# Two transformer blocks in split float32: which engine computes the weights' low parts, and how the account that orders the program treats VectorE and GpSimd

## The chip, the cores and the metric

One NeuronCore of a Trainium2 chip runs the whole program in one launch. The metric is the device time of one execution in microseconds (us), as the median of several runs. TensorE (PE) multiplies matrices, VectorE (DVE), ScalarE (ACT) and GpSimd (POOL) work elementwise, SyncE (SP) issues the transfers. Each engine takes its own instructions in the order in which the program lists them and waits on semaphores where it needs another's result. The program is unrolled: the order is fixed when the kernel is built.

## The reference

The input is 256 tokens of width 1024, float32. Two blocks of two layers follow each other; each layer is a SwiGLU feed-forward part (FFN, inner width 2816), a mixer, and a second FFN, each with an RMS norm ahead and a residual sum behind.

```python
for l in range(DEPTH):
    x = x + 0.5 * swiglu(rmsnorm(x, ffn1_norm[l]), ffn1_w_in[l], ffn1_w_out[l])
    x = x + hybrid_mixer(rmsnorm(x, mix_norm[l]), w_in[l], ...)
    x = x + 0.5 * swiglu(rmsnorm(x, ffn2_norm[l]), ffn2_w_in[l], ffn2_w_out[l])
```

The mixer of block 1 has two branches of 8 heads of 128: a gated delta rule in chunks of 64 tokens (a triangular system per chunk, then a state carried from chunk to chunk) and stick-breaking attention; each is multiplied by a branch matrix and gated, and their sum goes through `w_out`. The mixer of block 2 has three attention branches (latent, block-sparse, dilated). Every weight is used once, on all 256 tokens.

## The kernel before

**Split matmuls.** A float32 product is made of three one-pass matmuls: each operand is split into a high part `hi`, its rounding to TensorE's one-pass type, and a low part `lo = x - hi`; `mm3` issues hi·hi, hi·lo and lo·hi. So every weight that comes in (`raw`, by SP's transfers, four buffers) needs two elementwise instructions for each piece of 128x512 (some are narrower): the rounding `hi<-raw`, on ScalarE or VectorE, and the subtraction `lo<-raw,hi`. `Stream.split` (line 336) does it seven pieces ahead of their use (`PIECE_AHEAD`), into nine buffers. There are 1752 pieces. In `Net.split` (line 529) a table of costs decides the engines: the subtraction goes to GpSimd where that is reckoned to end earlier than on VectorE, or before TensorE's own time plus a slack: 7 us in the block-1 mixers (`POOL_SLACK`, line 21, set at lines 636 and 1491), 5 us at the end of an FFN (`EDGE_SLACK`, lines 22 and 679), 0 elsewhere. Data in PSUM (tiles `dn`, `acc`) never go to GpSimd.

**Dense and background work.** `dense` and `dense_tok` (one chunk of 256 weight columns, eight steps of 6 matmuls, 48 in all, into `dn` banks) are the program's thread. The mixers' chains, `delta` and `stick` in block 1, `soft2` and `soft3` in block 2, are generators that yield between steps; a step is some TensorE work into an `acc` bank and what the other engines do with it. After each eighth of a chunk `between` calls `tick` (line 492):

```python
if q and max(self.due.get(id(q), 0.0), self.nc.bank_free("acc", 4)) <= self.nc.free["tensor"]:
    self.step(q)
```

`due` is the time at which the chain's last step ends by the account in `Clock` (lines 233 to 289). The account keeps a time for each engine; it books each instruction behind its engine's last one, its inputs and its buffer, at the price of `cost`. So the account decides after how many dense matmuls a chain's next step stands in TensorE's queue. Where the program needs a chain's result, `need` and `drain` (lines 498 and 503) emit what is left of it at once, with no dense matmul between.

**A mixer of block 1** is 48 chunks: the columns for four pairs of heads (`dq`, `dk`, `dv`, `z`, `sq`, `sk`, `sv`, with the gates `ga` between), `gb`, then the branch matrices `yb` (four chunks, whose input `ob` needs all of `stick`: line 848) and `ya` (four chunks, input `oa`, all of `delta`: line 856), then `wo`. There are four `delta` chains in two lanes and four `stick` chains in one. By its dense matmuls the first mixer falls into four stages: pairs 0 and 1 (14 chunks), pairs 2 and 3 with the gates before them (16), the last gate, `z`, `gb` and `yb` (10), `ya` and `wo` (8).

Of the kernel before, what the change touches and what calls it, by code (L numbers as in the profile page):

```python
# [8 lines left out]
F = mybir.dt.float32  # L9
# [11 lines left out]
POOL_SLACK = 7.0  # L21
EDGE_SLACK = 5.0
# [210 lines left out]
class Clock:  # L233
    def __init__(self, nc):
        self.nc = nc
        self.free = {"tensor": 0.0, "vector": 0.0, "scalar": 0.0, "gpsimd": 0.0}
        self.ready = {}
        self.used = {}
        self.avail = {}
        self.slots = {}  # L240
        self.last = 0.0
        for n in self.free:
            setattr(self, n, Engine(self, n, getattr(nc, n)))
        self.sync = nc.sync
# [28 lines left out]

    def ends(self, eng, op, out, ins):

        at = max([self.free[eng], self.avail.get(out.tensor.name, 0.0)] + [self.ready.get(a.tensor.name, 0.0) for a in ins])
        return at + self.cost(eng, op, out, ins)

    def account(self, eng, op, aps, kw):
        out, ins = aps[0], aps[1:]  # L280
        cost = self.cost(eng, op, out, ins)
        at = max([self.free[eng], self.avail.get(out.tensor.name, 0.0)] + [self.ready.get(a.tensor.name, 0.0) for a in ins])
        end = at + cost
        self.free[eng] = end
        for a in aps:
            self.used[a.tensor.name] = end + 0.1
        self.ready[out.tensor.name] = end + (0.07 if eng == "tensor" else 0.13)
        if eng != "tensor":
            self.last = max(self.last, end + 0.13)
# [95 lines left out]
class Net:  # L385
    def __init__(self, ctx, tc, x, wsrc, small, out, parts):
# [16 lines left out]
        self.pool_slack = 0.0  # L403
# [125 lines left out]
    def split(self, hi, lo, x, gain=None):  # L529

        nc = self.nc
        if gain is None:
# [4 lines left out]
            psum = x.tensor.name.startswith(("dn_", "acc"))  # L537
            eng = "vector"
            if not psum and nc.ends("gpsimd", "tensor_sub", lo, [x, hi]) < max(
                    nc.ends("vector", "tensor_sub", lo, [x, hi]), nc.free["tensor"] + self.pool_slack):  # L540
                eng = "gpsimd"
            getattr(nc, eng).tensor_sub(lo, x, hi.bitcast(F))
# [82 lines left out]
    def dense(self, key, xs, mid=None):  # L625
# [10 lines left out]
        self.pool_slack = self.slack  # L636
# [35 lines left out]
    def ffn(self, part, nxt):  # L672
        nc = self.nc
# [3 lines left out]
        def out(c):  # L677
            if c == 10:
                self.pool_slack = EDGE_SLACK
# [804 lines left out]
    def run(self):  # L1484
        parts = self.parts
        for i, p in enumerate(parts):
# [4 lines left out]
            self.slack = POOL_SLACK if p[:2] == (1, "mix") else 0.0  # L1491
# [101 lines left out]
```

## Time and profile before

| | us |
|---|---|
| median of 3 runs (lowest, highest) | 2856.28 (2854.34, 2857.47) |
| the profiled execution, its own time | 2855.17 |
| its span, first to last instruction | 2853.4 |
| one mixer of block 1 (two of them) | 412.7 and 412.6 |
| one mixer of block 2 (two of them) | 262 |
| one FFN (eight of them) | 184 |

Times in the trace are counted from the span's start. A row's busy time is that in which an engine worked on an instruction; an engine whose instruction waits for a semaphore is idle, one whose instruction has begun is busy, whether it makes headway or not. All elementwise instructions pass through one helper and bear its line, 228, so they are told apart by their tiles. The granted clock is TensorE's, as a share of 2.4 GHz.

### The profile page before, as it was taken

Reading aid. Unit: us, or ns where it says so; the run is one execution under the profiler, and the core shown is the slowest. Engines: PE = TensorE matmul, PEld = TensorE weight load, DVE = VectorE, ACT = ScalarE, POOL = GpSimd, SP = SyncE. Lnnn points to the kernel's source line nnn. Section 1 sums busy time; section 2 is a strip of 40 time slices with the busy share of each in tenths; the row PEclk is TensorE's granted clock in tenths of the full one; section 3 lists DMA queues with packets and bytes.
Section 4 is the critical chain, followed back from the end, with each engine's and each line's share of the span. In section 5 each row is a group of like instructions: output and inputs, shape, how many; then the busy total and the mean of one; then the engine's idle time right before and its main releaser. Section 6 shows DMA issues by size and latency. Waiting matters only on the chain.

```text
span 2853.4 us, 57792 instructions
## 1 busy us (share of the span) xinstructions
PE 2701.7 (95%) x22692; PEld 2654.9 (93%) x22692; DVE 2067.7 (72%) x3749; ACT 1389.5 (49%) x2761; POOL 751.2 (26%) x625
## 2 busy tenths in 40 slices
PE   8997888999999978889999999899999999899998
PEld 8997887999999978889999999889999999889998
DVE  6678889476676688894766767766766767767766
ACT  5444454544454444545444544455544544545543
POOL 0016555770010265557600101322000002321000
PEclk9998999999999989999999999999999999999999
DMA  6553233345555532233455555434555554435553
GB/s 222 185 170 133 101 107 118 132 171 200 191 189 187 171 125 104 104 119 134 170 205 188 202 190 176 153 127 156 192 187 196 185 187 164 139 129 178 192 192 126
DMA packets 128146, 463.48 MB, mean 162 GB/s; under 512 B 14336, under 2 KB 14592, under 8 KB 127744
## 3 DMA queue, kind: packets, MB, share of 16 engines
q1 hardware_dynamic: 127872, 459.78, 47.5%
q8 instruction: 178, 2.92, 0.4%
q14 instruction: 96, 0.79, 0.1%
HBM read 458.67 MB, written 1.05 MB: 161 GB/s over the span
## 4 chain that ended last, share of the span: by engine, by line
PE 74%; DVE 20%; ACT 3%; issue 2%; DMA 1%; POOL 0%; DVEq 0%; SPq 0%; ACTq 0%; POOLq 0%
PE dn L228 53%; PE acc L228 21%; DVE ssum L228 2%; DVE lo L228 1%; DVE xl L228 1%; DVE d_N L228 1%; DVE hi L228 1%; DVE dq L228 1%; DVE dv L228 1%; DVE dk L228 1%; DVE d_prod L228 1%; DVE d_dec L228 1%; DVE d_Ub L228 1%; DVE d_P L228 1%; DMA raw<-in_w_dram 1%
## 5 line engine op out<-in xcount | busy, mean ns | idle before, releaser
L228 POOL TENSOR_TENSOR lo<-raw,hi 128x512 fp32r<-128x512 f32 (+2 forms) x502 | 665.2, 1345 | 1791.4 <-DVE lo L228 843.5
L228 ACT ACTIVATE hi<-raw 128x512 fp32r<-128x512 f32 (+2 forms) x1562 | 895.6, 617 | 333.3 <-PE dn L228 205.0
L228 DVE TENSOR_TENSOR lo<-raw,hi 128x512 fp32r<-128x512 f32 x1250 | 841.2, 710 | 166.9 <-ACT hi L228 155.9
L228 PE MATMUL dn<-xh,hi 128*128 128x256 f32 x4208 | 852.6, 284 | 6.0 <-DVE hi L228 6.0
L228 PE MATMUL dn<-xl,hi 128*128 128x256 f32 x4208 | 834.0, 280 | 4.1 <-DVE xl L228 4.1
L228 PE MATMUL dn<-xh,lo 128*128 128x256 f32 x4208 | 832.0, 279 | 4.7 <-DVE lo L228 4.7
L228 PEld LDWEIGHTS dn<-xh,hi 128*128 128x128 f32 x4208 | 647.3, 191 | 16.5 <-issue 9.1
L228 PEld LDWEIGHTS dn<-xl,hi 128*128 128x128 f32 x4208 | 646.7, 191 | 5.9 <-DVE xl L228 5.9
L228 PEld LDWEIGHTS dn<-xh,lo 128*128 128x128 f32 x4208 | 645.0, 191 | 5.5 <-DVE lo L228 5.5
L228 PE MATMUL acc<-al,hi 128*128 128x256 f32 x1408 | 204.3, 282 | 0.0
L228 PE MATMUL acc<-ah,hi 128*128 128x256 f32 x1408 | 202.8, 281 | 0.0
L228 PE MATMUL acc<-ah,lo 128*128 128x256 f32 x1408 | 202.8, 281 | 0.0
L228 ACT ACTIVATE ah<-us 128x512 fp32r<-128x512 f32 x88 | 55.7, 632 | 283.4 <-DVE us L228 283.4
L228 PEld LDWEIGHTS acc<-ah,lo 128*128 128x128 f32 x1408 | 183.0, 189 | 0.0
L228 PEld LDWEIGHTS acc<-al,hi 128*128 128x128 f32 x1408 | 183.0, 189 | 0.0
L228 PEld LDWEIGHTS acc<-ah,hi 128*128 128x128 f32 x1408 | 181.5, 188 | 0.0
L228 ACT ACTIVATE gs<-gs 128x512 f32<-128x512 f32 x88 | 55.9, 635 | 227.3 <-DVE gs L228 227.3
L228 PE MATMUL dn<-hi,xh 128*128 128x256 f32 (+2 forms) x640 | 139.7, 300 | 2.5 <-DVE k L228 2.5
L228 DVE TENSOR_TENSOR gs<-dn,nr 128x512 f32<-128x512 f32 x88 | 60.8, 691 | 103.1 <-PE dn L228 102.9
L228 DVE TENSOR_TENSOR us<-dn,nr 128x512 f32<-128x512 f32 x88 | 60.7, 690 | 102.7 <-PE dn L228 102.7
L228 PE MATMUL dn<-lo,xh 128*128 128x256 f32 (+2 forms) x640 | 130.8, 286 | 2.9 <-DVE lo L228 2.9
L228 PE MATMUL dn<-hi,xl 128*128 128x256 f32 (+2 forms) x640 | 130.9, 286 | 0.0
(319 smaller groups left out, 3234.2 us busy)
## 6 DMA issues: line engine op xcount, KB each, us to landing
raw<-in_w_dram SPq DMA_DIRECT2D x853, 512.0 KB, 4.3
raw<-in_w_dram SPq DMA_DIRECT2D x14, 384.0 KB, 3.2
raw<-in_w_dram SPq DMA_DIRECT2D x4, 408.0 KB, 4.0
cmat<-in_cmat_dram SPq DMA_DIRECT2D x1, 1216.0 KB, 6.9
x<-in_x_dram SPq DMA_DIRECT2D x4, 256.0 KB, 5.4
out_dram<-x SPq DMA_DIRECT2D x4, 256.0 KB, 2.6
cmat<-in_cmat_dram SPq DMA_DIRECT2D x1, 648.0 KB, 7.6
raw<-in_w_dram SPq DMA_DIRECT2D x2, 272.0 KB, 3.1
```

Of the source, the lines that this page charges most:

```text
L228: return f(*args, **kw)
```

## The change

Three things. `Net.split` gives every subtraction to VectorE; the two slacks go, and what set them. The account gets one more time, `port`: each instruction of GpSimd, and each of VectorE that touches no PSUM tile, begins no earlier than the last such instruction of either ended. The other choices by cost (rounding and copies between ScalarE and VectorE, additions between VectorE and GpSimd) are made by the same rules as before, on the new times.

```diff
--- before.py
+++ after.py
@@ -18,8 +18,6 @@
 EPS = 1e-6
 RAW, RAW_BUFS = 1024, 4
 PIECE, PIECE_AHEAD, PIECE_BUFS = 512, 7, 9
-POOL_SLACK = 7.0
-EDGE_SLACK = 5.0
 NORM_K = 6
 CP_A = 0.4
 HI_A = 0.3
@@ -238,7 +236,7 @@
         self.used = {}
         self.avail = {}
         self.slots = {}
-        self.last = 0.0
+        self.last = self.port = 0.0
         for n in self.free:
             setattr(self, n, Engine(self, n, getattr(nc, n)))
         self.sync = nc.sync
@@ -271,17 +269,25 @@
             return (0.055 if psum else 0.095) + n * 0.83e-3 + 0.093 * (len(ins) - 1)
         return 0.1 + n * {"tensor_scalar": 4e-3, "tensor_copy": 3.4e-3, "memset": 0.9e-3}.get(op, 2.2e-3)
 
+    def shared(self, eng, out, ins):
+
+        return eng == "gpsimd" or eng == "vector" and not any(
+            a.tensor.name.startswith(("dn_", "acc")) for a in [out] + ins)
+
+    def begins(self, eng, out, ins):
+        at = max([self.free[eng], self.avail.get(out.tensor.name, 0.0)] + [self.ready.get(a.tensor.name, 0.0) for a in ins])
+        return max(at, self.port) if self.shared(eng, out, ins) else at
+
     def ends(self, eng, op, out, ins):
 
-        at = max([self.free[eng], self.avail.get(out.tensor.name, 0.0)] + [self.ready.get(a.tensor.name, 0.0) for a in ins])
-        return at + self.cost(eng, op, out, ins)
+        return self.begins(eng, out, ins) + self.cost(eng, op, out, ins)
 
     def account(self, eng, op, aps, kw):
         out, ins = aps[0], aps[1:]
-        cost = self.cost(eng, op, out, ins)
-        at = max([self.free[eng], self.avail.get(out.tensor.name, 0.0)] + [self.ready.get(a.tensor.name, 0.0) for a in ins])
-        end = at + cost
+        end = self.ends(eng, op, out, ins)
         self.free[eng] = end
+        if self.shared(eng, out, ins):
+            self.port = end
         for a in aps:
             self.used[a.tensor.name] = end + 0.1
         self.ready[out.tensor.name] = end + (0.07 if eng == "tensor" else 0.13)
@@ -400,7 +406,6 @@
         self.bg = {"a": [], "b": [], "c": []}
         self.done = {}
         self.pending = []
-        self.pool_slack = 0.0
         self.due = {}
         self.consts()
 
@@ -534,12 +539,7 @@
                 nc.scalar.activation(hi, x, AF.Copy)
             else:
                 nc.vector.tensor_copy(hi, x)
-            psum = x.tensor.name.startswith(("dn_", "acc"))
-            eng = "vector"
-            if not psum and nc.ends("gpsimd", "tensor_sub", lo, [x, hi]) < max(
-                    nc.ends("vector", "tensor_sub", lo, [x, hi]), nc.free["tensor"] + self.pool_slack):
-                eng = "gpsimd"
-            getattr(nc, eng).tensor_sub(lo, x, hi.bitcast(F))
+            nc.vector.tensor_sub(lo, x, hi.bitcast(F))
         else:
             nc.scalar.activation(hi, x, AF.Copy, scale=gain)
             nc.vector.scalar_tensor_tensor(lo, x, gain, hi.bitcast(F), op0=OP.mult, op1=OP.subtract)
@@ -633,7 +633,6 @@
             self.mm3(lambda j: ps[j // 2][:, j % 2], w, (xs[0][k], xs[1][k]), range(n), lambda j: k == j % 2 == 0,
                      k == ch.kt - 1)
             self.between(k, mid)
-        self.pool_slack = self.slack
         return ps if n > 2 else ps[0]
 
     def between(self, k, mid):
@@ -675,8 +674,6 @@
         act = {}
 
         def out(c):
-            if c == 10:
-                self.pool_slack = EDGE_SLACK
             ch = self.W.get((part, "o", c))
             ah, al = act.pop(c)
 
@@ -1488,7 +1485,6 @@
             if i == 0:
                 self.load_x()
             self.load_consts(p[0])
-            self.slack = POOL_SLACK if p[:2] == (1, "mix") else 0.0
             self.sq_tag = lambda b, mix1=p[:2] == (1, "mix"): (f"d_P{b % 2}", 1) if mix1 else ("sq", 4)
             if p[1] == "mix":
                 with self.scope("mix"):
```

Of the instructions counted in the two programs: GpSimd's subtractions `lo<-raw,hi` go from 502 to 0 and `ml<-ma,mh` from 8 to 0, VectorE's from 1250 to 1752 and from 8 to 16. VectorE's `CAST hi<-raw` go from 190 to 113 and ScalarE's `hi<-raw` from 1562 to 1639. Within the first block-1 mixer, GpSimd gives up 171 `lo` (6 of them 272 wide) and 4 `ml`; its other instructions there, 20 products of `d_U` and 4 of `d_Ns` among them, 4 squares and 20 memsets, stay. VectorE gives 32 of 40 casts and 14 copies to ScalarE. TensorE's matmuls are the same; their order is not. SP's transfers are the same, in the same order.

VectorE at the start of the first mixer of block 1 (`xl` is the low part of the activations, `ssum` the sum of squares for the norm, `lo<-raw` a piece of the mixer's weights; the number behind a tile is its own), before:

```order
L228 SCALAR_TENSOR_TENSOR xl_13_84<-x_3_74,small,xh_8_79 128x256 x2
L228 SCALAR_TENSOR_TENSOR xl_14_85<-x_4_75,small,xh_9_80 128x256 x2
L228 SCALAR_TENSOR_TENSOR gqk_2587<-small 128x1
L228 TENSOR_TENSOR ssum<-d_P_471_2624 128x256
L228 TENSOR_TENSOR ssum<-ssum,d_P_475_2639 128x256 x2
L228 TENSOR_TENSOR ssum<-ssum,d_P_478_2653 128x256 x2
L228 TENSOR_TENSOR ssum<-ssum,d_P_482_2669 128x256 x2
L228 TENSOR_TENSOR lo_2674<-raw_2495,hi_2673 128x512
L228 TENSOR_TENSOR lo_2696<-raw_2547,hi_2695 128x512
L228 CAST hi_2725<-raw_2627 128x512
```

and now:

```order
L226 SCALAR_TENSOR_TENSOR xl_13_84<-x_3_74,small,xh_8_79 128x256 x2
L226 SCALAR_TENSOR_TENSOR xl_14_85<-x_4_75,small,xh_9_80 128x256 x2
L226 SCALAR_TENSOR_TENSOR gqk_2587<-small 128x1
L226 TENSOR_TENSOR lo_2615<-raw_2404,hi_2614 128x272
L226 TENSOR_TENSOR ssum<-d_P_471_2624 128x256
L226 TENSOR_TENSOR lo_2630<-raw_2433,hi_2629 128x512
L226 TENSOR_TENSOR ssum<-ssum,d_P_475_2639 128x256 x2
L226 TENSOR_TENSOR lo_2644<-raw_2433,hi_2643 128x512
L226 TENSOR_TENSOR ssum<-ssum,d_P_478_2653 128x256 x2
L226 TENSOR_TENSOR lo_2660<-raw_2495,hi_2659 128x512
L226 TENSOR_TENSOR ssum<-ssum,d_P_482_2669 128x256 x2
L226 TENSOR_TENSOR lo_2674<-raw_2495,hi_2673 128x512
```

The pieces that GpSimd had are in VectorE's queue, between the sums of squares.

TensorE in the last chunk of `gb`, ahead of `yb` (`obh`, `obl`: the stick branch's result), before (`d_P`, `d_T`, `d_N` are steps of a delta chain):

```order
L228 MATMUL dn_6664<-xl_12_83,hi_6517 128x256 x2
L228 MATMUL dn_6664<-xh_7_78,lo_6518 128x256 x2
L228 MATMUL acc_6712<-d_T_1279_6589,d_U_1222_6267 128x128 x2
L228 MATMUL dn_6664<-xh_8_79,hi_6542 128x256 x2
L228 MATMUL dn_6664<-xl_13_84,hi_6542 128x256 x2
L228 MATMUL dn_6664<-xh_8_79,lo_6543 128x256 x2
L228 MATMUL acc_6726<-d_N_1286_6625,d_Ns_1293_6655 128x128 x4
L228 MATMUL dn_6664<-xh_8_79,hi_6542 128x256 x2
L228 MATMUL dn_6664<-xl_13_84,hi_6542 128x256 x2
L228 MATMUL dn_6664<-xh_8_79,lo_6543 128x256 x2
L228 MATMUL dn_6664<-xh_9_80,hi_6568 128x256 x2
```

and now, directly ahead of the first matmul of `yb` (`b_qk` and `b_z` are stick's last steps):

```order
L226 MATMUL acc_6451<-d_T_1192_6228,d_N_982_5182 32x32 x8
L226 MATMUL acc_6462<-d_U_1148_6025,d_P_1228_6439 32x32 x8
L226 MATMUL acc_6500<-b_qk_6426,cmat 128x256
L226 MATMUL acc_6500<-b_qk_6426,ones 128x128
L226 MATMUL acc_6500<-b_qk_6426,cmat 128x128
L226 MATMUL acc_6505<-d_T_1192_6228,d_N_982_5182 64x64 x4
L226 MATMUL acc_6533<-ident,dv_4351 128x128 x4
L226 MATMUL acc_6541<-b_z_6211,sbv_5827 128x256
L226 MATMUL acc_6541<-b_z_6211,sbv_5827 128x128
L226 MATMUL acc_6541<-b_z_6211,sbv_5827 128x256
L226 MATMUL acc_6541<-b_z_6211,sbv_5827 128x128
L226 MATMUL dn_6553<-obh_454_2597,hi_6274 128x256 x2
```

Before, each step has dense matmuls before and behind it, and none of stick's stands here any more. Now stick's last three steps with TensorE work and five delta steps of the third pair stand together, with no dense matmul between; the first of either kind stand ahead of the rows shown.

TensorE directly ahead of the first matmul of `ya` (`oah`, `oal`: the delta branch's result), before:

```order
L228 MATMUL dn_6996<-obl_461_2604,hi_6927 128x256 x2
L228 MATMUL dn_6996<-obh_457_2600,lo_6928 128x256 x2
L228 MATMUL dn_6996<-obh_457_2600,hi_6927 128x256 x2
L228 MATMUL dn_6996<-obl_461_2604,hi_6927 128x256 x2
L228 MATMUL dn_6996<-obh_457_2600,lo_6928 128x256 x2
L228 MATMUL dn_7082<-oah_446_2589,hi_6945 128x256 x2
```

and now:

```order
L226 MATMUL acc_6999<-d_U_1275_6599,d_P_1328_6894 64x64 x4
L226 MATMUL acc_7007<-d_T_1333_6938,d_U_1275_6599 128x128 x2
L226 MATMUL acc_7013<-dq_5251,dk_5367 128x128 x4
L226 MATMUL acc_7020<-d_P_1346_7010,ktok_1153_6051 128x128 x2
L226 MATMUL acc_7024<-d_P_1346_7010,dk_5367 128x128
L226 MATMUL acc_7024<-d_P_1346_7010,dq_5251 128x128
L226 MATMUL acc_7024<-d_P_1346_7010,dk_5367 128x128
L226 MATMUL acc_7024<-d_P_1346_7010,dq_5251 128x128
L226 MATMUL acc_7033<-d_T_1333_6938,d_U_1275_6599 128x128 x2
L226 MATMUL acc_7037<-d_N_1344_7006,d_Ns_1348_7018 128x128 x4
L226 MATMUL acc_7060<-ident,d_dec_1353_7042 128x128 x4
L226 MATMUL dn_7084<-oah_446_2589,hi_6781 128x256 x2
```

Before, dense matmuls of `yb` lead straight into `ya`, and the last delta step (`ident,d_dec`) stands in the first chunk of `yb`. Now the last eight steps of the fourth delta chain stand behind the whole of `yb` in one row, and ahead of them the last step of the third.

## Rows read from the trace of the kernel before

**Rows 1.** The page: busy times, then three engines in 40 equal slices, busy tenths.
```profile
PE 2701.7 (95%) x22692; PEld 2654.9 (93%) x22692; DVE 2067.7 (72%) x3749; ACT 1389.5 (49%) x2761; POOL 751.2 (26%) x625
PE   8997888999999978889999999899999999899998
DVE  6678889476676688894766767766766767767766
POOL 0016555770010265557600101322000002321000
```

**Rows 2.** Busy time of every engine by stretch: stretch, length, busy us (count), granted clock.
```profile
198.40:323.50 125.10, 102.27 (x807) 100.51 (x806) 110.42 (x229) 62.56 (x157) 77.98 (x68) 0.89 0.36 122
323.50:478.80 155.30, 132.41 (x1095) 126.85 (x1094) 132.96 (x330) 74.78 (x180) 82.89 (x76) 0.96 0.33 111
478.80:565.40 86.60, 81.27 (x686) 79.29 (x685) 50.49 (x150) 43.08 (x81) 58.55 (x51) 0.96 0.35 119
565.40:611.10 45.70, 45.70 (x387) 45.70 (x386) 28.79 (x28) 16.46 (x31) 43.83 (x33) 1.00 0.49 168
981.60:1394.20 412.60, 363.53 (x2966) 354.68 (x2965) 322.64 (x734) 196.89 (x448) 263.84 (x226) 0.94 0.35 122
625.00:809.20 184.20, 183.15 (x1587) 182.93 (x1588) 128.87 (x204) 89.90 (x158) 10.47 (x8) 1.00 0.56 189
1776.30:2038.20 261.90, 251.83 (x2034) 239.80 (x2034) 190.69 (x324) 135.15 (x293) 64.56 (x48) 0.98 0.45 150
```

**Rows 3.** TensorE's waits: who for whom, us in total, times, longest us.
```profile
PE acc L228 <- DVE sbraw L228: 25.9, 7, 7.2
PE acc L228 <- DVE d_dec L228: 10.4, 6, 3.7
PE dn L228 <- DVE mqk L228: 12.7, 2, 6.3
```

**Rows 4.** Timeline, GpSimd above, VectorE below: start, us, engine, operation, count.
```profile
307.25 6.54 POOL L228 TENSOR_TENSOR lo<-raw,hi 128x512 fp32r<-128x512 f32 x5
...
308.81 1.28 DVE L228 SCALAR_TENSOR_TENSOR d_P<-d_N,ident 128x128 f32<-128x128 f32 x1
310.02 1.34 DVE L228 SCALAR_TENSOR_TENSOR d_P<-d_N,ident 128x128 f32<-128x128 f32 x1
```

**Rows 5.** Per tile, VectorE, first mixer of block 1: count, shortest/median/longest ns.
```profile
L228 DVE SCALAR_TENSOR_TENSOR d_N<-d_N,d_c,d_dec x16: 337/1366/1419, 264.5 to 482.5; 128x128 f32<-128x128 f32 x16
...
L228 DVE SCALAR_TENSOR_TENSOR dv<-pad,small,dv x24: 471/485/1536, 238.6 to 460.5; 128x256 f32<-128x256 f32 x24
...
L228 DVE STREAM_TRANSPOSE d_T<-d_U x24: 158/180/711, 307.5 to 522.1; 32x32 f32<-32x32 f32 x16, 128x512 f32<-128x512 f32 x8
```

**Rows 6.** Groups, same mixer: count, busy us, mean ns, then the idle time before.
```profile
L228 POOL TENSOR_TENSOR lo<-raw,hi 128x512 fp32r<-128x512 f32 x175 | 234.5, 1362 | 117.2 <-ACT hi L228 83.5 <-DVE hi L228 19.3 <-PE acc L228 7.6
...
L228 DVE CAST hi<-raw 128x512 fp32r<-128x512 f32 x42 | 34.7, 847 | 0.0
L228 DVE SCALAR_TENSOR_TENSOR dv<-pad,small,dv 128x256 f32<-128x256 f32 x24 | 20.7, 895 | 3.6 <-POOL pad L228 2.6 <-ACT dv L228 0.6
L228 DVE SCALAR_TENSOR_TENSOR d_N<-d_N,d_c,d_dec 128x128 f32<-128x128 f32 x16 | 15.9, 1053 | 0.0
```

**Rows 7.** Groups, VectorE, the FFN behind it: the same columns.
```profile
L228 DVE TENSOR_TENSOR lo<-raw,hi 128x512 fp32r<-128x512 f32 x125 | 81.2, 688 | 18.2 <-ACT hi L228 17.2
L228 DVE CAST hi<-raw 128x512 fp32r<-128x512 f32 x12 | 5.0, 417 | 0.0
```

**Rows 8.** Timeline: TensorE and VectorE at the end of the last delta chain.
```profile
528.78 0.68 PE L228 MATMUL acc<-d_U,d_P 128*64 128x64 f32 x8
530.20 0.61 PE L228 MATMUL acc<-d_T,d_U 128*128 128x128 f32 x4
...
546.27 0.60 PE L228 MATMUL acc<-ident,d_dec 128*128 128x128 f32 x4
...
548.58 0.75 DVE L228 SCALAR_TENSOR_TENSOR oal<-acc,small,oah 128x512 fp32r<-128x512 f32 x1 [1.60 <-ACT oah L228]
```

## The prediction

> **What bounds the kernel now.** I read the page's busy times and slices first, then the stretches, then who waits for whom, then single instructions. On the page TensorE is busy 95% of the span, VectorE 72%, GpSimd 26%, and GpSimd's work lies in two humps, at slices 3 to 9 and 14 to 20, where TensorE's digits fall from 9 to 7 and 8 [rows 1]. These are the two block-1 mixers. The stretches say the same in us [rows 2]: an FFN of 184.2 has TensorE busy for 183.2 and GpSimd for 10.5, so nothing is to be had there; a mixer of block 2 has 10 us of TensorE idle. The first block-1 mixer falls into stages of 125.1, 155.3, 86.6 and 45.7 us, 412.7 together (the second 412.6); TensorE is busy 102.3, 132.4, 81.3 and 45.7, at a granted clock of 0.89, 0.96, 0.96 and 1.00. So some 51 us per mixer are TensorE's idle time, and more goes to stretches at the lower of its two levels (1.2 of 2.4 GHz). Nearly all those waits are for VectorE: for the attention's raw tiles 25.9 us in the run, for delta's output 10.4 [rows 3]. The bound of these stages is thus VectorE being late, though it is busy only 110.4 of 125.1 and 133.0 of 155.3 us.
>
> Why it is late stands in the timeline [rows 4]: GpSimd does five subtractions in 6.54 us, 1.3 each, and in that time VectorE's 128x128 products take 1.28 and 1.34 us. The same operation is not long by itself: sixteen of the similar `d_N` have a shortest of 337 ns and a median of 1366, `dv` runs from 471 to 1536 [rows 5]. VectorE's instruction waits for one whole GpSimd instruction, inside its own busy time. Operations that read PSUM or transpose show none of it: 24 transposes stay at or under 711 ns [rows 5].
>
> **The change, part by part.** All terms are for one block-1 mixer, against the profiled execution (2855.17 us; the median of the runs is 1.1 above it).
>
> *Subtractions to VectorE.* GpSimd's subtractions in the window, 175 of 1.36 us [rows 6], go to VectorE at 81.2 / 125 = 0.65 us each [rows 7]: +114 us of VectorE work.
>
> *What no longer blocks.* Casts cost 34.7 us where 42 x 0.417 = 17.5 would do [rows 6, 7]; `dv` 20.7 against 24 x 0.485 = 11.6, `d_N` 15.9 against 16 x 0.337 = 5.4 [rows 5, 6]. These three give 37 us. The same difference over all of VectorE's groups in the mixer comes to about 96 us. Bounds: 37 from these alone, 117 if every GpSimd subtraction blocked VectorE for half its length (234.5 / 2). I take 96. GpSimd was busy for 263 us over the four stages [rows 2]; less the subtractions of [rows 6] and four of `ml` of like length, some 23 us of products, squares and memsets stay, so up to 23 may still block; I take 12.
>
> *Casts and copies to ScalarE.* 32 casts at 0.417 [rows 7] and 14 copies, some 6 us: -19 us on VectorE, +25 on ScalarE, which is busy for 197 of 413 us in the mixer [rows 2]. It hides there.
>
> Sum: 322.7 - 96 + 12 + 114 - 19 = 334; counted instruction by instruction in the new order, each at its unblocked duration, 306 + 12 = 318. Both say: **VectorE's load does not fall; it moves.** By stages I count 72, 123, 67 and 44 us (plus the 12, mostly in the second), where it is 110, 133, 50 and 29 now [rows 2]. The last two stages have the room: they are 86.6 and 45.7 us long.
>
> *Stage 1* (125.1 us). TensorE's work at the full clock is about 102.3 x 0.89 = 91, less 3 for chain steps that now stand later. VectorE needs 72 and no longer decides. The norm and the gates of delta still make TensorE wait, some 10 us. I take 98; bounds 88 (TensorE alone) and 112 (half the gain).
>
> *Stage 2* (155.3 us). TensorE needs 132.4 x 0.96 = 127, VectorE 123 + 8. With waits of either for the other, and one place where the second stick chain is called for and six background steps stand in a row (some 5 us), I take 142; bounds 131 and 155.
>
> *Stage 3* (86.6 us). TensorE needs 81.3 x 0.96 = 78, less 4 for steps moved past its end. New are two places at which chains are emitted to their end with nothing between: ahead of `yb` and ahead of `ya`. Ahead of `ya` stand eight delta steps; before, the same stretch took from 528.8 to 549.3, 20.5 us, with dense matmuls between [rows 8]. Alone I estimate 15 us, of which 6 are TensorE's own work: 10 us idle, between 4 (the steps need no more than their matmuls and a little) and 15. Ahead of `yb` VectorE has some 14 us of work to do in the row: 10 us idle, between 5 and 15. Who waits: TensorE itself, in order, with the branch matmuls behind; ScalarE and VectorE only until the nine piece buffers are full. I take 74 + 20 = 94, with 2 for the lower clock behind the waits: 96; bounds 83 and 106.
>
> *Stage 4* stays at 46: TensorE is busy throughout and VectorE gets 44 us of work at most.
>
> Sum: 98 + 142 + 96 + 46 = 382, **-30 us per mixer**, -60 for two.
>
> *Elsewhere.* In a block-2 mixer and at an FFN's ends a few subtractions move (some 40 and 4): 0.65 us each is added, about as much blocking goes. The one long wait there, 6.3 us twice for `mqk` [rows 3], ends with a PSUM reader behind a queue of VectorE work, and may go either way. Zero, between -8 and +8 in all. SP's transfers keep their order; `raw` comes free earlier, as a subtraction takes half the time.
>
> The Trainium skill, in Perfetto Trace Analysis, section Optimizing Scalar/DVE Operations, says that with a saturated VectorE it may make sense to give work to ScalarE or even GpSimd, and in the same place that the last might not help, since the two share an SBUF port. By the first half this change is wrong, and a mixer would grow by the 114 us less the 19: VectorE at 418 us. The rows decide for the second half here: an instruction of 0.34 us that takes 1.37.
>
> **The rivals.**
>
> 1. *The two forced rows grow* (slower). The account books GpSimd and VectorE one behind the other, even for transposes and reductions, which the trace shows unblocked [rows 5]. So it takes VectorE for later than it is, emits steps later than needed, and more of each chain is left for the rows ahead of `yb` and `ya`. Together they hold 17 steps. The first two stages give 40 us; the mixer is slower from the point where the rows cost TensorE 12.6 + 40 = 53 us idle, 3.1 us a step. Against it: the old chain took 2.5 us a step with dense work between [rows 8]. For it: TensorE's longest wait on such a step was 3.7 us for `d_dec` and 7.2 for the raw tiles [rows 3]. At 3.7 us a step the mixer takes 10 us more: 2875. In the Trainium skill, SBUF — State Buffer, section Who interferes with whom, reductions never contend and two-input SBUF operations do so only with a GpSimd instruction that reads SBUF; by that rule the account is indeed too strict, and memsets and transposes would not have to be kept apart. Chance 0.11.
>
> 2. *VectorE becomes the bound* (slower). If the blocking were only another name for waits that come back elsewhere, VectorE would need 418 us in a mixer of 412.7: with 6 us of waits 424, and 2878. It decides if less than about 80 of the 96 us come back. Against it: GpSimd has only 23 us left there to block with. Chance 0.04.
>
> 3. *No change.* Stage 2 at its upper bound (155) and stage 3 at 106, so that they give back what stage 1 gains: 98 + 155 + 106 + 46 = 405, and the block-2 mixers lose 4 us each: 2848; with stage 1 at 102 it is 2856. It needs VectorE's in-order queue to be late for other reasons than GpSimd. Chance 0.09.
>
> 4. *More than forecast.* The rows cost half, stage 1 comes down to TensorE's 88 and stage 2 to 131: 88 + 131 + 88 + 46 = 353, or 2736. Chance 0.09.
>
> **How the numbers follow.** My forecast, 2855 - 60 + 1 = 2796 us against the median, with 2750 to 2848 around it, has a chance of 0.67. The first two rivals add 0.15 on the slower side. A measurement can tell 0.2%, 5.7 us, from no change. So faster by more: 0.67 + 0.09, and a third of the third rival, 0.79; within: 0.06; slower: 0.15. The range leaves out the far half of rival 4 and most of rivals 1 and 2: 2748 to 2864.
>
> **What would show it.** In the profile after: VectorE's busy time near 2050 us and GpSimd's under 120; `d_N` with a median near 340 ns and `dv` without long ones; the first stage near 98 us with TensorE's clock above 0.95; TensorE's waits on the raw tiles gone. Against that, TensorE idle for some 10 us directly ahead of `yb` and again ahead of `ya`, and VectorE busy in the fourth stage. The prediction is wrong if the mixers' first stage stays over 112 us (then GpSimd wasn't what delayed VectorE), or if the two rows cost more than 40 us per mixer.

## The result and the profile after

The changed kernel takes 2792.19 us (median of 4 runs, 2791.08 to 2794.54); the kernel before, on the same chip, 2856.57 (2854.34 to 2857.47). The ratio is 0.9777, interval 0.976 to 0.9794: 64 us less. The forecast was 2796.

The page of the changed kernel, busy times, three engines in 40 slices, and the shares of the chain that ended last; the last line has these shares for the kernel before:

```profile
PE 2687.7 (96%) x22692; PEld 2644.8 (95%) x22692; DVE 2051.2 (74%) x4163; ACT 1438.2 (52%) x2870; POOL 75.7 (3%) x106
...
PE   8999799899999997998999999999999999999998
...
DVE  7668878676676788886767767767767767767766
...
POOL 0000001100000001010000000000000000000000
...
PE 86%; DVE 8%; ACT 3%; issue 2%; DMA 1%; DVEq 0%; SPq 0%; POOL 0%; ACTq 0%
...
PE 74%; DVE 20%; ACT 3%; issue 2%; DMA 1%; POOL 0%; DVEq 0%; SPq 0%; ACTq 0%; POOLq 0%
```

GpSimd's two humps of [rows 1] are gone, and VectorE is busy for 16 us less than before although it does 510 subtractions more. The chain that ended last spends 8% on VectorE where it spent 20% before, and 86% on TensorE (74%).

The first block-1 mixer of the changed kernel by the four stages of [rows 2], same columns (stretch, length, busy us and count of PE, PEld, DVE, ACT, POOL, granted clock, share and rate of the transfers):

```profile
194.20:287.50 93.30, 88.39 (x735) 88.06 (x733) 79.28 (x178) 65.44 (x162) 3.65 (x9) 0.96 0.50 165
287.50:432.90 145.40, 128.94 (x1098) 125.59 (x1096) 122.54 (x374) 79.69 (x184) 13.79 (x23) 0.94 0.33 109
432.90:537.70 104.80, 91.41 (x756) 87.03 (x755) 81.15 (x262) 51.18 (x111) 14.22 (x16) 0.91 0.34 116
537.70:584.50 46.80, 46.80 (x387) 46.80 (x387) 34.69 (x57) 24.88 (x45) 0.00 (x0) 0.97 0.49 161
```

Together 390.3, where [rows 2] have 412.7. Stage 1 gains 31.8 us, stage 2 9.9; stage 3 gives back 18.2, stage 4 1.1. Mind the counts: stage 1 holds 72 matmul instructions fewer than before, stage 3 70 more. Steps have moved from one to the other, so a stage's gain is not the effect of one cause.

VectorE's instructions by tile, first mixer (`d_N`) and whole run (`dv`, `sbraw`; the last line is `sbraw` in the kernel before): count, shortest/median/longest ns.

```profile
L226 DVE SCALAR_TENSOR_TENSOR d_N<-d_N,d_c,d_dec x16: 342/344/347, 272.9 to 473.4; 128x128 f32<-128x128 f32 x16
...
L226 DVE SCALAR_TENSOR_TENSOR dv<-pad,small,dv x48: 443/482/486, 230.4 to 1175.3; 128x256 f32<-128x256 f32 x48
...
L226 DVE TENSOR_TENSOR sbraw<-sbraw,b_rs x8: 691/691/693, 246.3 to 1202.9; 128x512 f32<-128x512 f32 x8
...
L228 DVE TENSOR_TENSOR sbraw<-sbraw,b_rs x8: 1665/1709/1733, 258.4 to 1272.3; 128x512 f32<-128x512 f32 x8
```

The long ones of [rows 5] are gone. TensorE's longest waits in the changed kernel (us in total, times, longest):

```profile
PE acc L226 <- ACT b_z L226: 23.8, 4, 9.4
PE acc L226 <- DVE d_dec L226: 9.0, 2, 4.5
PE acc L226 <- DVE b_ss L226: 8.0, 2, 4.0
PE acc L226 <- DVE b_qk L226: 6.9, 2, 3.5
```

`sbraw` and `mqk` of [rows 3] are not among them. In their place stand steps of the chains, `b_z` first.

To tell where the 64 us come from I cut the span at the first matmul of each norm's sum. So counted, a block-1 mixer goes from 413.8 to 390.1 and 389.3 us (the second was 413.8 too), which makes 48 of 64; the rest of the program goes from 2025.8 to 2009.9.

### The profile page after: what moved, and what is told of

It is laid out like the page before. It is cut to its first block, busy times and chain, and to the rows that moved or that the text cites. A ratio compares the mean times of both kernels' runs of the same rounds, so it can differ in the third digit from the quotient of the medians.

```text
span 2789.3 us, 57423 instructions
## 1 busy us (share of the span) xinstructions
PE 2687.7 (96%) x22692; PEld 2644.8 (95%) x22692; DVE 2051.2 (74%) x4163; ACT 1438.2 (52%) x2870; POOL 75.7 (3%) x106
## 4 chain that ended last, share of the span: by engine, by line
PE 86%; DVE 8%; ACT 3%; issue 2%; DMA 1%; DVEq 0%; SPq 0%; POOL 0%; ACTq 0%
PE dn L226 62%; PE acc L226 24%; DVE lo L226 3%; DMA raw<-in_w_dram 1%; ACT hi L226 1%; DVE d_prod L226 0%; DVE d_rows L226 0%; DVE dq L226 0%; ACT b_tm L226 0%; DVE d_dec L226 0%; DVE dk L226 0%; DVE d_Ub L226 0%; DVE pad L226 0%; DVE b_qk L226 0%; DVE d_Nb L226 0%
## 5 line engine op out<-in xcount | busy, mean ns | idle before, releaser
L226 DVE TENSOR_TENSOR lo<-raw,hi 128x512 fp32r<-128x512 f32 x1752 | 1148.9, 692 | 225.7 <-ACT hi L226 208.0
L226 ACT ACTIVATE hi<-raw 128x512 fp32r<-128x512 f32 (+1 forms) x1639 | 933.6, 617 | 265.6 <-PE dn L226 165.2
L226 PE MATMUL dn<-xh,hi 128*128 128x256 f32 x4208 | 842.6, 281 | 6.2 <-DVE hi L226 6.0
L226 PEld LDWEIGHTS dn<-xh,hi 128*128 128x128 f32 x4208 | 640.4, 189 | 16.3 <-issue 9.1
L226 PEld LDWEIGHTS dn<-xl,hi 128*128 128x128 f32 x4208 | 639.6, 189 | 5.8 <-DVE xl L226 5.6
L226 DVE TENSOR_TENSOR al<-us,ah 128x512 fp32r<-128x512 f32 x88 | 60.9, 692 | 61.4 <-ACT ah L226 61.4
```

The source lines that it names most:

```text
L226: return f(*args, **kw)
```

## The experiments

All times are medians; ratios are to the kernel before, timed on the same chip in the same session.

### Which engine, or which order

The first kernel has the old order on every queue, and only the engine of the subtractions changes: the old choice is still made and booked, and VectorE does the work.

```diff
-            getattr(nc, eng).tensor_sub(lo, x, hi.bitcast(F))
+            nc.account(eng, "tensor_sub", [lo, x, hi.bitcast(F)], {})
+            nc.nc.vector.tensor_sub(lo, x, hi.bitcast(F))
```

> Every subtraction on VectorE, but each engine's queue keeps the order of the kernel before: the old account and the old choice are still booked, only the instruction itself goes to VectorE. Theory (blocking: the gain comes from GpSimd's reading subtractions no longer holding VectorE): most of the gain stays, 2800 to 2825 us, d_N with a median under 400 ns. Rival (order: the gain comes from the account's later places for the background steps): no gain, 2845 us or more, with TensorE waiting for VectorE as before.

The second has the new order, and GpSimd does the pieces that it did before (`on_pool` looks them up in a list of the 1752 pieces), while the account books VectorE.

```diff
-            nc.vector.tensor_sub(lo, x, hi.bitcast(F))
+            nc.account("vector", "tensor_sub", [lo, x, hi.bitcast(F)], {})
+            on = nc.nc.gpsimd if self.on_pool(x) else nc.nc.vector
+            on.tensor_sub(lo, x, hi.bitcast(F))
...
```

> The order of the changed kernel on every engine, but the 502 weight subtractions and 8 of ml that GpSimd had before are issued on GpSimd again. Theory (blocking): VectorE's short products take 1.3 us again and most of the gain is lost, 2825 to 2865 us. Rival (order): the gain stays, 2790 to 2805 us.

Measured: with the old order and VectorE 2798.47 us, ratio 0.9804 (0.9788 to 0.982); with the new order and GpSimd 2865.32, ratio 1.0034 (1.0021 to 1.0047). So the engine alone gives 57 of the 64 us, and the order alone loses 10. The mixers show how the two go together: 392.7 and 395.0 us in the first kernel, 422.5 and 419.1 in the second. The new order costs 5 to 9 us per mixer while GpSimd subtracts and saves 3 to 6 when it doesn't.

The page of the kernel with the new order and GpSimd, busy times, and two of its tiles on VectorE, with `b_rs` of the changed kernel as the last line:

```profile
PE 2712.0 (95%) x22692; PEld 2660.7 (93%) x22692; DVE 2007.6 (70%) x3653; ACT 1439.1 (50%) x2870; POOL 732.1 (26%) x616
```

```profile
L227 DVE TENSOR_TENSOR b_rs<-b_rs,nr x8: 166/1221/1278, 256.7 to 1265.8; 128x8 f32<-128x8 f32 x8
L227 DVE TENSOR_TENSOR sbraw<-sbraw,b_rs x8: 691/1200/1720, 258.0 to 1267.1; 128x512 f32<-128x512 f32 x8
...
L226 DVE TENSOR_TENSOR b_rs<-b_rs,nr x8: 166/166/169, 246.1 to 1202.7; 128x8 f32<-128x8 f32 x8
```

With the same instructions in the same order, VectorE does 510 subtractions fewer than in the changed kernel and is busy for 43.6 us less. What they are worth, the row of the subtractions in the changed kernel tells (count, busy us, mean ns):

```profile
L226 DVE TENSOR_TENSOR lo<-raw,hi 128x512 fp32r<-128x512 f32 x1752 | 1148.9, 692 | 225.7 <-ACT hi L226 208.0
```

That is 1148.9 / 1752 = 0.66 us of busy time each (less than the mean of 0.69, as some overlap), some 334 us for 510. So some 290 us, 0.57 us for each piece that GpSimd took, went into waiting inside other instructions. Among them are short ones of the chains: `b_rs`, 128x8, takes 1221 ns (the median) instead of 166, and `sbraw`, for which TensorE waits, follows it.

Not all of the 73 us between these two kernels need be this waiting. TensorE's waits for GpSimd's own `lo`, in the kernel with the new order and GpSimd and then in the kernel before:

```profile
PE dn L227 <- POOL lo L546: 14.6, 6, 6.5
...
PE dn L228 <- POOL lo L228: 0.9, 2, 0.4
```

With the new order GpSimd's pieces themselves come late for TensorE; the likely reason, not tried, is that the account takes them to be on VectorE. In the kernel before they hardly did, so the lateness of GpSimd's own results is not what the change took away.

The stretches of that kernel and of the one with the old order on VectorE, stage 1, stage 2, stages 3 and 4:

```profile
196.50:297.20 100.70, 90.50 (x735) 89.39 (x733) 74.91 (x120) 60.97 (x152) 68.92 (x59) 0.95 0.45 145
297.20:456.80 159.60, 136.46 (x1096) 130.98 (x1095) 121.89 (x325) 83.35 (x191) 79.68 (x76) 0.90 0.32 105
456.80:619.00 162.20, 142.59 (x1140) 137.23 (x1139) 100.89 (x244) 76.41 (x157) 108.66 (x92) 0.91 0.36 118
```

```profile
194.20:309.80 115.60, 100.36 (x806) 98.61 (x806) 102.26 (x283) 63.23 (x159) 6.73 (x13) 0.91 0.41 133
309.80:454.50 144.70, 127.94 (x1094) 122.49 (x1093) 127.07 (x384) 74.64 (x180) 14.81 (x25) 1.00 0.37 119
454.50:587.20 132.70, 126.97 (x1070) 124.11 (x1069) 106.30 (x253) 60.46 (x112) 8.81 (x10) 0.99 0.42 139
```

The shape over the stages comes from the order: with GpSimd back, stage 1 is 100.7 us long all the same, and with the old order and no blocking it is 115.6. The sum comes from the engine.

### Does a GpSimd instruction block by reading?

Two kernels leave the changed program as it is and give GpSimd an extra piece of work for each of the 502 pieces that it had: to repeat the subtraction into the raw tile, which nobody reads any more, or to write zeros over that tile twice.

```diff
...
+            if x.tensor.name.startswith("raw"):
+                self.nsub += 1
+                if OLD[self.nsub - 1] == "1":
+                    nc.nc.gpsimd.tensor_sub(x, x, hi.bitcast(F))
```

(in the other kernel the last line is `for _ in range(2): nc.nc.gpsimd.memset(x, 0.0)`).

> The changed kernel; GpSimd does the same 502 weight subtractions once more behind VectorE's, into the raw tile, which nobody reads any more. Nobody waits for their result but the next load of that tile. Theory (blocking by GpSimd's reads of SBUF): VectorE's two-input products take 1.3 us again and the time rises by 30 to 70 us, to 2820 to 2860. Rival (order): within 8 us of 2792.

> The changed kernel; in place of each repeated subtraction GpSimd writes zeros twice over the raw tile (about 1.1 us together), reading nothing. If only GpSimd instructions that read SBUF hold up VectorE's two-input products: within 8 us of 2792 and d_N near 340 ns. If any GpSimd instruction does: 2815 us or more, d_N with a median of 0.8 us or more.

Measured: 3066.98 us with the repeated subtraction, ratio 1.0744 (1.0728 to 1.076), 275 us over the changed kernel; 2808.83 with the memsets, ratio 0.9838 (0.9824 to 0.9853), 16.6 over it. The first is far beyond what I had put down; the second lies between its two cases. Rows of the kernel with the repeated subtraction, its busy times, then two tiles from 200 to 600 us, then the subtractions `lo` on VectorE in the whole run:

```profile
PE 2773.9 (90%) x22692; PEld 2707.0 (88%) x22692; DVE 2375.1 (77%) x4163; ACT 1437.7 (47%) x2870; POOL 829.8 (27%) x608
```

```profile
L227 DVE SCALAR_TENSOR_TENSOR d_N<-d_N,d_c,d_dec x16: 339/346/1392, 309.2 to 568.8; 128x128 f32<-128x128 f32 x16
...
L227 DVE STREAM_TRANSPOSE d_T<-d_U x19: 158/201/712, 382.9 to 595.7; 32x32 f32<-32x32 f32 x12, 128x512 f32<-128x512 f32 x7
...
L227 DVE TENSOR_TENSOR lo<-raw,hi 128x512 fp32r<-128x512 f32 x1752 | 1320.8, 792 | 213.0 <-ACT hi L227 190.4
```

The same 4163 VectorE instructions take 324 us longer, 0.65 us for each repeated subtraction; 172 of the 324 lie in VectorE's own subtractions, 1320.8 us where it was 1148.9. Transposes stay at 712 ns at most, `d_N` goes up to 1392. Here nothing is taken off VectorE, so the whole price shows; in the kernel before, the subtractions that VectorE was spared hid most of it. Some of the 275 us is another thing: the raw tile is held until GpSimd is done. The memsets hold it too.

Rows of the kernel with the memsets: `d_N` in the first mixer, the casts of the run, GpSimd's group:

```profile
L227 DVE SCALAR_TENSOR_TENSOR d_N<-d_N,d_c,d_dec x16: 343/346/350, 274.6 to 481.8; 128x128 f32<-128x128 f32 x16
...
L227 DVE CAST hi<-raw x113: 414/418/686, 5.4 to 2782.3; 128x512 fp32r<-128x512 f32 x113
...
L549 POOL MEMSET raw<- 128x512 f32 (+2 forms) x1004 | 510.0, 521 | 1994.1 <-DVE lo L227 1964.1
```

GpSimd is busy for 510 us more and no `d_N` is longer than 350 ns; VectorE's busy time is that of the changed kernel, 2050.5. A long two-input instruction that is left there, `d_prod` (its median is 191 ns), lies beside a product on GpSimd that does read SBUF:

```profile
289.41 1.31 POOL L227 TENSOR_TENSOR d_Ns<-d_N,cmat 128x512 f32<-128x512 f32 x1
289.49 1.30 DVE L227 TENSOR_TENSOR d_prod<-d_rows,d_Ub 128x60 f32<-128x60 f32 x1
```

So of the two the repeated subtraction, which reads, blocks `d_N`, and the memset does not; other kinds of GpSimd instruction were not tried. The block-1 mixers still take 7 to 8 us more each. ScalarE and VectorE wait 93.7 us in the run for raw tiles to arrive, where it is 59.1 in the changed kernel: the held tile is the likely cause, though nothing else was tried on it. With the repeated subtraction they wait 146.0 us, so how much of its 275 us the held tile makes is not shown. By the Trainium skill, SBUF — State Buffer, section Who interferes with whom, a VectorE operation with two SBUF inputs contends with a GpSimd instruction that reads SBUF, not with one that only writes. The two kernels agree, for `d_N`: 1392 against 350 ns at the most.

### The two halves of the change as it is written

First all subtractions on VectorE, with the account as it was, so without the turns by which GpSimd and VectorE are booked one behind the other:

```diff
-        return max(at, self.port) if self.shared(eng, out, ins) else at
+        return at
```

> The first half of the change alone: every subtraction of a weight's high part on VectorE, and the account lets VectorE and GpSimd work side by side as it did before. Its emission has one row of forced stick steps (12 chunk openings in a row ahead of yb) where the changed kernel has two. My theory (the time comes from GpSimd no longer blocking VectorE, the order is worth little): within 12 us of the changed kernel, 2780 to 2804. Rival (the rule of turns in the account earns a part by itself, because it makes the stick steps due later and so spares TensorE waits): at least 2806.

Then the account with turns, and the old choice of engine, with both slacks, put back:

```diff
-            nc.vector.tensor_sub(lo, x, hi.bitcast(F))
+            psum = x.tensor.name.startswith(("dn_", "acc"))
+            eng = "vector"
+            if not psum and nc.ends("gpsimd", "tensor_sub", lo, [x, hi]) < max(
+                    nc.ends("vector", "tensor_sub", lo, [x, hi]), nc.free["tensor"] + self.pool_slack):
+                eng = "gpsimd"
+            getattr(nc, eng).tensor_sub(lo, x, hi.bitcast(F))
...
```

> The second half alone: the account takes turns, and the old choice between VectorE and GpSimd stands; booked that way it gives GpSimd some 204 of the 502 subtractions. My theory (cost goes with the number of subtractions on GpSimd): 204 of 502 leave about 0.4 of the 57 to 64 us in place, so 2814 to 2822 and, with its forced row of 16 openings ahead of yb, up to 2832. Rival 1 (the rule of turns alone is what gains, by placing those subtractions where VectorE is free): at most 2800. Rival 2 (a subtraction on GpSimd costs as long as any is left in the stage): 2845 or more.

Measured: 2793.34, ratio 0.9778 (0.9764 to 0.9793), the changed kernel's own; and 2809.0, ratio 0.9832 (0.9817 to 0.9846). So the account's turns aren't needed once VectorE has all subtractions. With the choice left in, GpSimd keeps 204 of its 502 subtractions and 17 of the 64 us are missing, less than the 22 to 30 that I had put down. Its mixers are 402.5 us, and TensorE waits there for `d_T` up to 14.8 us at a stretch. Outside of them it is 7 us shorter than the changed kernel, 1.0 to 1.3 us in five of the eight FFNs, although GpSimd does 54 of the 204 there. Either not every subtraction on GpSimd costs time, or this order wins more than they cost; neither was tried.

### The time won outside the block-1 mixers

The changed kernel's order, with GpSimd taking back the 148 subtractions that the list has outside these mixers (the edit against the kernel with the new order and GpSimd):

```diff
...
-            return OLD[self.nsub - 1] == "1"
-        return name.startswith("ma") and self.mix1_now
+            return OLD[self.nsub - 1] == "1" and not self.mix1_now
+        return False
...
```

> The changed kernel's emission, with GpSimd taking back only the 148 subtractions that it had outside the two block-1 mixers (154 of the kernel before, less the 6 that sit at an edge): at the FFNs' starts and ends and in the block-2 mixers. The prediction put their effect at nothing. Theory (a subtraction on GpSimd costs about the same anywhere, because VectorE is stopped and the cover there is thinner than I thought): the 16 us that the change gained outside these mixers come back, 2803 to 2814. Rival (those 16 us come from the new emission, for instance from the weights' tiles being asked for earlier): within 5 us of the changed kernel, 2787 to 2797.

Measured: 2798.78 us, ratio 0.9798 (0.9785 to 0.9811): 6.6 of the 16 us come back, between the two cases. The waits of this kernel have a row of [rows 3] again, unchanged:

```profile
PE dn L227 <- DVE mqk L227: 12.7, 2, 6.3
```

So the long wait in each block-2 mixer is GpSimd's doing. The length of the wait is not its price, though: the two waits make 12.7 us, and the two mixers are together 3.7 us longer than in the changed kernel (259.7 and 260.9 against 259.6 and 257.3). With all 510 back in the same order, the parts outside are 10.7 us longer than in the changed kernel; the remaining 5 go with the old order while GpSimd subtracts (with all of them on VectorE the old order costs nothing there: 2009.1 against 2009.9). Which instructions make it, stays open.

### The forced rows

The account's turns narrowed to VectorE operations with two SBUF inputs, copies and `tensor_scalar`, and to GpSimd instructions other than memsets:

```diff
...
+        mats = [a for a in ins if len(a.shape) > 2 or a.shape[-1] > 1]
+        if eng == "gpsimd":
+            return op != "memset"
+        return eng == "vector" and not any(a.tensor.name.startswith(("dn_", "acc")) for a in [out] + ins) and (
+            len(mats) > 1 or op in ("tensor_copy", "tensor_scalar"))
...
```

> The changed kernel, with the account's rule of turns narrowed to what the trace showed as blocked: VectorE operations with two SBUF inputs or copies, and GpSimd operations that read. The emission has no forced row of more than 11 openings. Theory (the forced rows cost the waits at them, 9.4 us at the second stick chain and about 9 at yb and ya in each of two mixers, and lower the clock in the third stage): 20 to 35 us less than the changed kernel, 2757 to 2775. Rival (what the rows waited for is late anyway, and the wait only moves to the next step of the stick chain): 2784 to 2800.

And the changed account, with steps emitted when they are due within 2 us:

```diff
-            if q and max(self.due.get(id(q), 0.0), self.nc.bank_free("acc", 4)) <= self.nc.free["tensor"]:
+            if q and max(self.due.get(id(q), 0.0), self.nc.bank_free("acc", 4)) <= self.nc.free["tensor"] + 2.0:
```

> The changed kernel, but a stick step is emitted as soon as it is due within 2 us of TensorE's account, not once it is due. No forced row of more than 11 openings is left. Theory (forced rows cost as above): 2757 to 2780. Rival (TensorE now stands up to 2 us ahead of each of some 17 steps of two chains in two mixers): 2800 to 2830.

Measured: 2794.02, ratio 0.9778 (0.9762 to 0.9795), no gain; and 2816.92, ratio 0.9861 (0.9846 to 0.9875). The narrowed account spreads the row ahead of `ya`, but leaves eleven openings ahead of `yb` (an opening is the first matmul of a step into an `acc` bank) and the place of the second stick chain. TensorE waits about as long as before at each: 8.9 us at the second stick chain, 3.3 and 4.2 ahead of `yb`, and 4.5 for `d_dec` ahead of `ya`. The earlier emission dissolves all of them: the block-1 mixers then take 387.4 and 386.7 us, 2.7 less, and the block-2 mixers 273.1 and 275.1 where it was 259.6 and 257.3. The forecast of 12 to 35 us from the rows failed: what TensorE waits for is late whether the steps stand in a row or not.

### Earlier emission in the block-1 mixers alone

Steps are emitted 2 us early in these mixers, and elsewhere as in the changed kernel:

```diff
...
-            if q and max(self.due.get(id(q), 0.0), self.nc.bank_free("acc", 4)) <= self.nc.free["tensor"]:
+            if q and max(self.due.get(id(q), 0.0), self.nc.bank_free("acc", 4)) <= self.nc.free["tensor"] + self.early:
...
+            self.early = 2.0 if p[:2] == (1, "mix") else 0.0
```

> The changed kernel with steps emitted when due within 2 us of TensorE's account, in the block-1 mixers alone. The kernel that did so everywhere lost 13 to 18 us in each block-2 mixer and won 2.6 to 2.7 us in each block-1 mixer against the changed kernel. Theory (the two add up place by place): 2784 to 2789. Rival (the loss in the block-2 mixers was an effect of the earlier stages on what weights are in flight, and follows): 2800 or more.

The same with `begins` returning `at`, so without turns, and that with 4.0 in place of 2.0:

> As before, and with the account's turns taken out as well, so every subtraction on VectorE, no turns, and 2 us of earliness in block 1. Without turns the block-2 mixers took 2.3 us less together and the block-1 mixers 4 us more. Theory (the earliness replaces what the turns did in block 1): 2781 to 2788. Rival (the two block-1 emissions differ and the turns earn their 4 us there): 2788 to 2794.

> As the one before, with 4 us of earliness in block 1. Theory (TensorE stands at each step emitted early, up to 2 us more for some 17 steps of the stick chains in a mixer, with the dense work behind it not lost but later): 2 to 15 us more than with 2 us of earliness, 2785 to 2800. Rival (the step was late anyway, and the row ahead of yb vanishes further): up to 8 us less, 2774 to 2781.

Measured: 2785.36 us (2783.28 to 2789.95), ratio 0.9753 (0.974 to 0.9766); without turns 2814.3, 0.9852 (0.9837 to 0.9867); with 4 us 2855.15, 0.9987 (0.9978 to 0.9996). The first is where it was expected, 7 us under the changed kernel, though the two were not timed side by side and their intervals overlap. The other two missed by 26 and 55 us: their mixers are 401 and 420 to 421 us long.

TensorE in the first mixer from norm to norm, the changed kernel and then the version with 2 us:

```profile
205.00:595.10 390.10, 355.34 (x2967) 347.28 (x2966) 316.24 (x865) 220.60 (x494) 31.51 (x46) 0.94 0.40 133
```

```profile
206.20:593.00 386.80, 354.42 (x2966) 343.55 (x2965) 313.54 (x862) 219.19 (x493) 31.32 (x46) 0.98 0.41 134
```

Its idle time is 32.4 us instead of 34.8: but for one of 4.5 us at the start, which both have, the few long waits became many of at most 2.7 us. The granted clock is 0.98 instead of 0.94, and yet TensorE is busy for only 0.9 us less; why is open. The waits of the version without turns and with 4 us, in the whole run:

```profile
PE acc L226 <- DVE d_rows L226: 19.3, 4, 5.2
PE acc L226 <- DVE d_T L226: 15.8, 13, 2.5
PE dn L226 <- DVE lo L226: 14.0, 4, 4.4
```

There TensorE is idle for 53 us in the first mixer, mostly at steps of the chains. My reading, which no kernel tests by itself: it has reached these steps too soon. The turns make the account reckon VectorE later than it is; against that, 2 us of earliness are about right, and without the turns they are too much. Turns with 4 us were not run in these mixers.

## Why the prediction was right, and where it was off

**The cause was right.** `d_N` was forecast at a median near 340 ns and has 344; `dv` has no long ones; VectorE's busy time was to be near 2050 and is 2051.2, GpSimd's under 120 and is 75.7; TensorE's waits on `sbraw` are gone. VectorE's load in the mixer was forecast to move and not to fall, 318 to 334 us; it is 317.7. That GpSimd, not the order, had delayed VectorE is shown by the pair of kernels that change one of them each. By stages the load was put at 72, 123, 67 and 44 us (plus 12) and is 79, 123, 81 and 35: less of it than forecast reaches the last stage.

**Stage 1 (98; 93.3).** The step "less 3 for chain steps that now stand later" was too small: TensorE's work there is 88.39 x 0.96 = 85 us at the full clock against 91, so 6 went, and idle time is 4.9, not 10. The lower clock, put at nothing, costs 3. My test of the cause by this stage ("wrong if it stays over 112") was a poor one: with GpSimd's subtractions back it would have passed, at 100.7, and with the old order and no blocking it would have failed, at 115.6.

**Stage 2 (142; 145.4).** The 142 are 127 of TensorE's work and 15 of waits. The work is 128.94 x 0.94 = 121 us at the full clock, 6 less, and the lower clock, put at nothing, costs the other 8. The waits are 16.5 us, near the 15, but by luck: the place where the second stick chain is called for was put at 5 us and the timeline of TensorE there shows 14.6, so all the others, put at 10, make 2:

```profile
317.36 0.39 PE L226 MATMUL dn<-lo,xh 128*128 128x256 f32 x2
327.19 2.93 PE L226 MATMUL acc<-b_z,sbv 128*128 128x256 f32 x8 [9.44 <-ACT b_z L226]
329.91 1.91 PE L226 MATMUL acc<-d_T,d_Ns 128*128 128x128 f32 x8
332.61 1.13 PE L226 MATMUL acc<-d_U,d_P 128*128 128x128 f32 x8 [0.78 <-ACT d_P L226]
337.65 0.84 PE L226 MATMUL acc<-d_T,d_N 128*32 128x32 f32 x16 [3.92 <-DVE b_ss L226]
338.91 0.32 PE L226 MATMUL acc<-d_U,d_P 128*32 128x32 f32 x2 [0.42 <-ACT d_P L226]
```

**Stage 3 (96; 104.8).** Here the term failed that says "less 4 for steps moved past its end". Steps came in: 756 matmul instructions instead of 686, and 91.41 x 0.91 = 83 us at the full clock instead of 78. So 5 us more, not 4 less: 9 too few. The two rows were put at 20 us of idle time and the stage has 13.4, 6.1 ahead of `yb` and 7.3 ahead of `ya`: 6.6 too many. The lower clock was put at 2 and costs 91.4 - 83 = 8.4: 6.4 too few. Together that is the 8.8 by which the stage is longer.

```profile
476.11 1.19 PE L226 MATMUL acc<-b_qk,cmat 128*128 128x256 f32 x2 [3.42 <-DVE b_qk L226]
...
486.66 1.65 PE L226 MATMUL acc<-b_z,sbv 128*128 128x256 f32 x4 [2.25 <-ACT b_z L226]
...
536.88 1.17 PE L226 MATMUL acc<-ident,d_dec 128*128 128x128 f32 x4 [4.51 <-DVE d_dec L226]
```

The three places together were forecast at 25 us and have 28. But they are not a price of the rows, as I had it: dissolved, they leave 32.4 us of idle time in the mixer against 34.8.

**Stage 4 (46; 46.8).** As forecast, with VectorE at 35 us and not 44.

The work at the full clock in these accounts is an estimate, busy time times mean granted clock. The four stages hold the same matmuls in both kernels, and the products add up to 342 us before and 335 now, so each of these terms is uncertain by some us. The price of the lower clock is not shown either: with the clock at 0.98 in the version with 2 us of earliness, TensorE's busy time in the mixer is all but the same.

**The mixers (-30; -24 each, from norm to norm)** and **elsewhere (0, between -8 and +8; -16).** The mixers came out 12 us longer than forecast and the rest 16 us shorter, twice its bound. The two errors cancel to 4 us: that 2796 lies so near 2792 is luck. Elsewhere the step "about as much blocking goes" was wrong, and so was leaving `mqk` open: the 148 subtractions there cost 6.6 us of the run by themselves, the `mqk` waits with them; where the rest of the 16 comes from is only narrowed down.

**The rivals.** Rows that grow: TensorE waited 9.4 us for one step, more than the 3.7 and 7.2 I judged by, but for 28 us in all, not 53. VectorE as the bound: its load is 318 of 390 us. No change: it needed another cause than GpSimd. More than forecast: stage 1 went half the way from 98 to its 88, stages 2 and 3 went the other way.

## What to carry to other kernels

Before work is given to GpSimd because VectorE is late, look in the trace at the shortest and the longest of one VectorE instruction: if the long ones coincide with GpSimd reading SBUF, the offload takes back inside other instructions what it spares (here 0.57 of 0.66 us a piece), short instructions of a chain among them. Judge such a change by a kernel that moves the work and keeps the order, and one that keeps the work and moves the order; the length of one stage tells nothing when steps move between stages. And a long wait is no price of the place where it stands until a kernel without that place has been timed.

## What the runs showed of the hardware

- A VectorE instruction of 128x8 elements goes from 166 to a median of 1221 ns beside GpSimd's subtractions, and `d_N`, 128x128, from 344 to 1366: what is added doesn't go with the instruction's own size.
- A subtraction repeated on GpSimd costs VectorE 0.65 us of its busy time and the program 0.55 (the held raw tile included); a pair of memsets over the same tile leaves `d_N` at 350 ns at the most, and takes a cast from 418 to 686 ns at the most.
